# Applying dt with the mask in the scan of a hybrid decoder layer: three multiplications take other places

## The chip, the cores and the metric

The kernel runs on one core of a Trainium2 chip. The metric is device time in microseconds (us), the median of several executions; one further execution was profiled.

## The reference, cut to what matters

The layer is a feed-forward block, a mixer and a second feed-forward block, each followed by a layer norm, on 512 tokens of 1024 channels. The mixer runs sliding-window attention beside a state-space scan. Only the scan is touched. It has 4 groups of 8 heads, 64 channels a head, and goes through the tokens in 4 chunks of 128:

```python
xdt = (x * dt[..., None]).reshape(b, nc, CHUNK, G, K, P)
CB = jnp.einsum("bclgn,bcsgn->bcgls", Cc, Bc)
y_diag = jnp.einsum("bcgls,bcgkls,bcsgkp->bclgkp", CB, Lmat, xdt)
decay_states = jnp.exp(A_cum[..., -1:] - A_cum)
states = jnp.einsum("bclgn,bcgkl,bclgkp->bcgkpn", Bc, decay_states, xdt)
...
u = (y.reshape(b, L, D_INNER) * jax.nn.silu(z)).reshape(b, L, N_SSM_GROUPS, -1)
u = u * lax.rsqrt(jnp.mean(jnp.square(u), axis=-1, keepdims=True) + RMS_EPS)
u = u.reshape(b, L, D_INNER) * norm_w
y_ssm = u @ w_ssm_branch
```

So dt is a factor for each source token and head, the root is a factor for each token and group, and norm_w is a factor for each channel.

## The kernel before, in words

Every large product is computed in three matmuls of high and low halves (`mm3`, lines 124 to 126), so TensorE (PE) does three passes of 512 columns for each 128x128 block of weights. For each weight tile a copy on ScalarE (ACT) makes the high half `wh` (line 99) and a subtraction on VectorE (DVE) the low half `wl` (line 100); four buffers of each run ahead of PE.

The scan of group g is a generator, `ssd(g)`, that `weave` slips between the weight tiles of other products ("mains"): after a main, one step of the scan is issued. A step is either `decays(c)` or `turn(c - 1)` with `products(c)` and `lead(c + 1)`; so about one main, or two, lies between the decays of a chunk and its products. Each engine works its own queue strictly in the order that the scheduler of the language writes down at build time; `issue_after` keeps the scan's instructions behind the main's last matmul.

For a chunk c of a group:

- `lead` makes `ud` on GpSimd (POOL), four operations (line 572), from which PE makes the decays' exponents (lines 583 and 584).
- `decays` takes their exponentials on ACT into two tiles `seg` of four heads each (line 586), forms `cb`, the masked product of C and B (line 591), multiplies both `seg` by `cb` on DVE (line 593), makes `xdt` on DVE (line 595), and on POOL `yx` (x times d_skip, line 597) and `xds` (`xdt` times the decay to the chunk's end, line 601).
- `products` does eight matmuls of `seg` and `xdt`, one a head (line 609), then the products with the state (lines 615 and 621), adds all up on DVE, takes the sum of squares on ACT (line 632), the power -1/2 on POOL (line 634, the root `rs`), and multiplies `yx` by the root and by `normB`, norm_w broadcast to all partitions (line 635).
- `turn` transposes `yx` on PE (line 642) and splits it into the halves of `uT`, one copy on ACT and one subtraction on DVE for all four 128-column blocks (line 643 through `split_act`, lines 144 and 145). `w_ssm_tiles` multiplies `uT` by its weights later.

Tiles in PSUM for these steps come from one pool, `sm`, of four buffers. Below, "group 1, chunk 3" counts both from 0.

Of the kernel before, what the change touches and what calls it, by code (L numbers as in the profile page):

```python
# [39 lines left out]
def hybrid_layer(  # L40
# [247 lines left out]
    with tc.tile_pool(name="mix", bufs=1) as mix:  # L288
# [89 lines left out]
        with tc.tile_pool(name="attn", bufs=1) as ap:  # L378
# [37 lines left out]
            dAf = dA.rearrange("p c h -> p (c h)")  # L416
            for i, m in enumerate((upper, lower, ones)):
                nc.tensor.matmul(ps[:, i * P:(i + 1) * P], m, dAf, start=True, stop=True)
            decf = dec.rearrange("p a c h -> p (a c h)")
            nc.scalar.activation(decf, ps[:, :384], AF.Exp)  # L420
            nc.vector.tensor_scalar_mul(decf[:, :256], decf[:, :256], 0.5)
# [116 lines left out]
            k_tile(1)  # L538
            side = attention()
# [7 lines left out]
        with tc.tile_pool(name="ssd", bufs=1) as sp:  # L547
            ysum = sp.tile([P, 8, SEQ], F32, name="ysum")

            def ssd(g):  # L550
# [4 lines left out]
                normB = sp.tile([P, 512], F32, name="normB", bufs=1)  # L555
                nc.gpsimd.dma_start(normB, norm_w[0, g * 512:(g + 1) * 512].partition_broadcast(P))

                def hb(ap):
                    return ap.unsqueeze(2).broadcast_to([P, HPG, HD])

                def hv(ap):
                    return ap.rearrange("p (h d) -> p h d", h=HPG)
# [14 lines left out]
                def decays(c):  # L577
# [14 lines left out]
                    for seg in segs:  # L592
                        nc.vector.tensor_tensor(seg, seg, cb.unsqueeze(1).broadcast_to([P, 4, P]), ALU.mult)
                    xdt = sp.tile([P, 512], F32, name="xdt", bufs=2)
                    nc.vector.tensor_tensor(hv(xdt), hv(xn[:, c]), hb(dth[:, c, hs]), ALU.mult)
# [3 lines left out]
                    if c + 1 < NT:  # L599
                        xds = sp.tile([P, 512], F32, name="xds", bufs=1)  # L600
                        nc.gpsimd.tensor_tensor(hv(xds), hv(xdt), hb(dec[:, 1, c, hs]), ALU.mult)
                    st[c].update(segs=segs, xdt=xdt, yx=yx, xds=xds)

                def products(c):
                    tok = slice(c * P, (c + 1) * P)
                    segs, xdt, yx, xds = (st[c][k] for k in ("segs", "xdt", "yx", "xds"))
                    py = sm()
                    for h in range(HPG):
                        nc.tensor.matmul(py[:, h * HD:(h + 1) * HD], segs[h // 4][:, h % 4], xdt[:, h * HD:(h + 1) * HD],
                                         start=True, stop=True)  # L610
# [24 lines left out]
                    nc.vector.scalar_tensor_tensor(yx, yx, rs[:, 1:2], normB, ALU.mult, ALU.mult)  # L635

                def turn(c):
# [5 lines left out]
                    split_act((uT[:, :, 0, tok], uT[:, :, 1, tok]), ps.rearrange("p (i t) -> p i t", i=4))  # L643
# [93 lines left out]
```

## Time and profile before

| what | value |
|---|---|
| time, median of 3 runs | 1451.63 us (1449.44 to 1453.68) |
| the profiled execution's own time | 1453.2 us |
| its span, first to last instruction | 1451.5 us |
| PE busy | 1426.5 us, 98% of the span |
| DVE busy | 791.5 us, 55% |
| ACT busy | 482.1 us, 33% |
| POOL busy | 195.3 us, 13% |

The span is what the trace covers; the own time is 1.7 us longer, for what lies around the instructions. Busy times of the engines overlap. A PE that is busy for 98% leaves little room: only what the other engines make PE wait, and a lower clock of PE, can be given back.

### The profile page before, as it was taken

The page shows a single profiled execution, that of the slowest core. Times are in us where ns is not written, and L with a number is a line of the kernel's source. Part 1 is how long each engine was busy: PE and PEld are TensorE (multiplying, and loading weights), DVE is VectorE, ACT ScalarE, POOL GpSimd, SP SyncE. Part 2 cuts the span into 40 slices and gives each one's busy share as a digit, 9 for nine tenths or more (in the row PEclk, how much of TensorE's full clock was granted, in tenths as well). Part 3 has the DMA queues.
Part 4 walks back from the last instruction along what each step waited for, and adds up shares of the span by engine and source line. Part 5 has one row for each costly group of instructions (what it writes and reads, how often), then busy time and mean ns, then how long its engine had stood idle before and what let it go on. Part 6 is the DMA issues. An engine that isn't in the chain of part 4 may idle for free. (4 is left out here: it accounts for less than half of the span.)

```text
span 1451.5 us, 17121 instructions
## 1 busy us (share of the span) xinstructions
PE 1426.5 (98%) x6700; PEld 1169.7 (81%) x6700; DVE 791.5 (55%) x1246; ACT 482.1 (33%) x789; POOL 195.3 (13%) x214
## 2 busy tenths in 40 slices
PE   8999999999999999999999999999999999999997
PEld 6888888888877777887888888878878888888885
DVE  4343343233867884358659588686574434433235
ACT  4232232121346775223444234223313322322220
POOL 1000000000000000245244154261110000000001
PEclk9999999999999999999999999999999999999999
DMA  8433333323422133641231322345735333333321
GB/s 273 121 88 102 98 90 102 99 89 105 138 81 72 45 86 108 199 119 56 80 87 59 95 73 74 95 124 161 222 110 181 95 102 95 95 102 93 97 87 58
DMA packets 195633, 154.46 MB, mean 106 GB/s; under 512 B 6532, under 2 KB 169424, under 8 KB 195552
## 3 DMA queue, kind: packets, MB, share of 16 engines
q1 hardware_dynamic: 188608, 130.17, 30.1%
q0 software_dynamic: 6944, 23.19, 5.0%
q8 instruction: 53, 0.87, 0.3%
q14 instruction: 28, 0.23, 0.0%
HBM read 140.76 MB, written 12.58 MB: 106 GB/s over the span
## 5 line engine op out<-in xcount | busy, mean ns | idle before, releaser
L100 DVE TENSOR_TENSOR wl<-raw,wh 128x1024 fp32r<-128x1024 f32 (+1 forms) x233 | 299.6, 1287 | 417.3 <-ACT wh L99 412.6
L99 ACT CAST wh<-raw 128x1024 fp32r<-128x1024 f32 (+1 forms) x233 | 244.3, 1050 | 694.4 <-issue 323.7
L124 PE MATMUL acc<-xT,wh 128*128 128x512 f32 (+2 forms) x1120 | 441.9, 395 | 0.0
L125 PE MATMUL acc<-xT,wh 128*128 128x512 f32 (+2 forms) x1120 | 434.8, 388 | 0.0
L126 PE MATMUL acc<-xT,wl 128*128 128x512 f32 (+2 forms) x1120 | 433.8, 387 | 0.0
L124 PEld LDWEIGHTS acc<-xT,wh 128*128 128x128 f32 x1120 | 210.9, 188 | 44.5 <-issue 3.2
L125 PEld LDWEIGHTS acc<-xT,wh 128*128 128x128 f32 x1120 | 210.7, 188 | 44.2 <-issue 3.3
L126 PEld LDWEIGHTS acc<-xT,wl 128*128 128x128 f32 x1120 | 210.4, 188 | 43.0 <-issue 0.2
L124 PE MATMUL dn<-wh,hT 128*128 128x512 f32 x352 | 137.2, 390 | 0.0
L125 PE MATMUL dn<-wl,hT 128*128 128x512 f32 x352 | 137.1, 390 | 0.0
L126 PE MATMUL dn<-wh,hT 128*128 128x512 f32 x352 | 136.9, 389 | 0.0
L160 POOL TENSOR_TENSOR sts<-sts,cols 128x1 f32<-128x1 f32 x12 | 11.9, 990 | 719.9 <-DVE sts L159 719.9
L572 POOL TENSOR_TENSOR ud<-upper,dAr 128x512 fp32r<-128x512 f32 x64 | 86.4, 1378 | 104.2 <-PE sm L584 104.2
L239 DVE TENSOR_TENSOR t<-t,acc 128x512 f32<-128x512 f32 x44 | 30.2, 687 | 111.6 <-PE acc L126 111.4
L125 PEld LDWEIGHTS dn<-wl,hT 128*128 128x128 f32 x352 | 66.1, 188 | 13.7
L126 PEld LDWEIGHTS dn<-wh,hT 128*128 128x128 f32 x352 | 66.1, 188 | 13.6
L124 PEld LDWEIGHTS dn<-wh,hT 128*128 128x128 f32 x352 | 66.1, 188 | 13.6
L124 PE MATMUL z<-wh,xT 128*128 128x512 f32 x128 | 51.5, 402 | 0.0
L124 PE MATMUL acc<-uT,wh 128*128 128x512 f32 x128 | 50.5, 395 | 0.0
L126 PE MATMUL z<-wh,xT 128*128 128x512 f32 x128 | 49.9, 390 | 0.0
L125 PE MATMUL z<-wl,xT 128*128 128x512 f32 x128 | 49.9, 390 | 0.0
L126 PE MATMUL acc<-uT,wl 128*128 128x512 f32 x128 | 49.9, 390 | 0.0
(212 smaller groups left out, 1691.8 us busy)
## 6 DMA issues: line engine op xcount, KB each, us to landing
raw<-in_w_in_dram SPq DMA_DIRECT2D x66, 512.0 KB, 3.7
raw<-in_ffn_w_gate_dram SPq DMA_DIRECT2D x44, 512.0 KB, 3.8
raw<-in_ffn_w_up_dram SPq DMA_DIRECT2D x44, 512.0 KB, 3.7
raw<-in_ffn_w_down_dram SPq DMA_DIRECT2D x44, 512.0 KB, 3.6
raw<-in_w_ssm_branch_dram SPq DMA_DIRECT2D x16, 512.0 KB, 3.4
raw<-in_w_attn_branch_dram SPq DMA_DIRECT2D x8, 512.0 KB, 4.1
raw<-in_w_out_dram SPq DMA_DIRECT2D x8, 512.0 KB, 4.4
r<-in_x_dram SPq DMA_DIRECT2D x8, 256.0 KB, 5.7
```

The costliest lines, as they stand in the source:

```text
L99: nc.scalar.copy(h[:, :n], raw[:, :n])
L100: nc.vector.tensor_tensor(l[:, :n], raw[:, :n], f(h[:, :n]), ALU.subtract)
L124: nc.tensor.matmul(ps, lh, rh, start=start, stop=False)
L125: nc.tensor.matmul(ps, lh, rl, start=False, stop=False)
L126: cur["mm"] = nc.tensor.matmul(ps, ll, rh, start=False, stop=stop)
L160: nc.gpsimd.tensor_tensor(mv[:, 3:4], mv[:, 2:3], mhalf[:, 0:1], ALU.pow)
L239: nc.vector.tensor_tensor(t, t, pu, ALU.mult)
L572: nc.gpsimd.tensor_tensor(ud[:, i], upper.unsqueeze(1).broadcast_to([P, 4, P]), f(dAr[:, i, c, h0:h0 + 4]).unsqueeze(2).broadcast_to([P, 4 ...
```

## The change

Three multiplications of the scan move. First, dt: `xdt` is no longer made. The eight heads' masks are multiplied one by one by dt (a factor of each partition) and by `cb` in one DVE instruction a head, and the matmuls take `xn` itself; the factor that `xds` needs goes into `dec[:, 1]` once, ahead of the scan. Second, norm_w: its four broadcast loads are gone; its 16 rows of 128 are loaded once in the attention stage, transposed by PE and kept as columns (`nwc`), and `turn` multiplies by a column while it splits, so the one copy and one subtraction of 512 columns become four of each of 128. Third, the root: `yx` is multiplied by it on ACT instead of on DVE.

```diff
+            rows = ap.tile([P, SEQ], F32, tag="ta", name="ta", bufs=2)
+            nc.gpsimd.dma_start(rows[:16, :P], norm_w[0].rearrange("(t p) -> t p", p=P))
...
-            nc.vector.tensor_scalar_mul(decf[:, :256], decf[:, :256], 0.5)
+            nc.vector.tensor_scalar_mul(dec[:, 0], dec[:, 0], 0.5)
+            nc.vector.scalar_tensor_tensor(dec[:, 1], dec[:, 1], 0.5, dth, ALU.mult, ALU.mult)
...
+            nwc = heads[:, 0]
+            ps = sm()
+            with tc.issue_after(cur["mm"].ins):
+                nc.tensor.transpose(ps[:, :16], rows[:16, :P], ident[:16, :16])
+            nc.scalar.copy(nwc[:, :16], ps[:, :16])
...
-                normB = sp.tile([P, 512], F32, name="normB", bufs=1)
-                nc.gpsimd.dma_start(normB, norm_w[0, g * 512:(g + 1) * 512].partition_broadcast(P))
...
-                    for seg in segs:
-                        nc.vector.tensor_tensor(seg, seg, cb.unsqueeze(1).broadcast_to([P, 4, P]), ALU.mult)
-                    xdt = sp.tile([P, 512], F32, name="xdt", bufs=2)
-                    nc.vector.tensor_tensor(hv(xdt), hv(xn[:, c]), hb(dth[:, c, hs]), ALU.mult)
+                    for h in range(HPG):
+                        s_, h_ = segs[h // 4][:, h % 4], g * HPG + h
+                        nc.vector.scalar_tensor_tensor(s_, s_, dth[:, c, h_:h_ + 1], cb, ALU.mult, ALU.mult)
...
-                        nc.gpsimd.tensor_tensor(hv(xds), hv(xdt), hb(dec[:, 1, c, hs]), ALU.mult)
+                        nc.gpsimd.tensor_tensor(hv(xds), hv(xn[:, c]), hb(dec[:, 1, c, hs]), ALU.mult)
...
-                        nc.tensor.matmul(py[:, h * HD:(h + 1) * HD], segs[h // 4][:, h % 4], xdt[:, h * HD:(h + 1) * HD],
+                        nc.tensor.matmul(py[:, h * HD:(h + 1) * HD], segs[h // 4][:, h % 4], xn[:, c, h * HD:(h + 1) * HD],
                                          start=True, stop=True)
...
-                    nc.vector.scalar_tensor_tensor(yx, yx, rs[:, 1:2], normB, ALU.mult, ALU.mult)
+                    nc.scalar.activation(yx, yx, AF.Copy, scale=rs[:, 1:2])
...
-                    split_act((uT[:, :, 0, tok], uT[:, :, 1, tok]), ps.rearrange("p (i t) -> p i t", i=4))
+                    for i in range(4):
+                        w_, p_ = nwc[:, 4 * g + i:4 * g + i + 1], ps[:, i * P:(i + 1) * P]
+                        nc.scalar.activation(uT[:, i, 0, tok], p_, AF.Copy, scale=w_)
+                        nc.vector.scalar_tensor_tensor(uT[:, i, 1, tok], p_, w_, f(uT[:, i, 0, tok]), ALU.mult, ALU.subtract)
```

In the changed kernel's lines, 578 is the `ud` of line 572, 592 the exponentials of 586, 597 the `cb` of 591, 600 the new mask multiplication, 602 and 606 the `yx` and `xds` of 597 and 601, 637 to 639 the sum of squares to the root of 632 to 634, 640 the multiplication by the root on ACT, 650 and 651 the two halves of the split.

The scheduler also writes down another order at some places. Three of them matter.

The first is POOL's queue where the scan goes from group 1 to group 2. Before, the root of group 1's chunk 2 (`rs_5246`) stands ahead of the four `ud` of group 2's chunk 0:

```order
L597 TENSOR_TENSOR yx_5322<-xn_3350,heads_66 128x512
L634 TENSOR_TENSOR rs_5246<-rs_5246,cols_90 128x1
L572 TENSOR_TENSOR ud_5618<-upper_74,dAr_2621 128x512 x2
L572 TENSOR_TENSOR ud_5621<-upper_74,dAr_2621 128x512 x2
L597 TENSOR_TENSOR yx_5676<-xn_4977,heads_66 128x512
```

In the changed kernel the same root is `rs_5274`:

```order
L602 TENSOR_TENSOR yx_5354<-xn_3356,heads_66 128x512
L578 TENSOR_TENSOR ud_5660<-upper_74,dAr_2621 128x512 x2
L578 TENSOR_TENSOR ud_5663<-upper_74,dAr_2621 128x512
L639 TENSOR_TENSOR rs_5274<-rs_5274,cols_90 128x1
L578 TENSOR_TENSOR ud_5663<-upper_74,dAr_2621 128x512
L602 TENSOR_TENSOR yx_5722<-xn_4985,heads_66 128x512
```

The root moved behind three of the four `ud`; the same happens from group 0 to group 1 and from group 2 to group 3.

The second is ACT's queue at the same point, group 1's chunk 3. Before, the sum of squares of chunk 2 is followed by the exponentials of chunk 3:

```order
L632 ACTIVATE yo_5247,rs_5246<-yx_5169 128x512
L302 ACTIVATE BT_5289<-acc_5264,cols_90 128x512
L326 COPY xn_4977<-sm_5298 128x4x128
L586 ACTIVATE seg_5307<-sm_5304 128x512
L586 ACTIVATE seg_5312<-sm_5309 128x512
L99 CAST wh_5477<-raw_5475 128x1024
```

In the changed kernel the multiplication by that root stands between them:

```order
L637 ACTIVATE yo_5275,rs_5274<-yx_5191 128x512
L302 ACTIVATE BT_5317<-acc_5292,cols_90 128x512
L326 COPY xn_4985<-sm_5326 128x4x128
L640 ACTIVATE yx_5191<-yx_5191,rs_5274 128x512
L592 ACTIVATE seg_5335<-sm_5332 128x512
L592 ACTIVATE seg_5340<-sm_5337 128x512
L307 ACTIVATE th_5322<-BT_5317 128x512
L99 CAST wh_5551<-raw_5549 128x1024
```

The multiplication, which needs POOL's root, moved in ahead of chunk 3's exponentials.

The third is DVE's queue in group 3, from chunk 1's multiplication by z (line 629, now 634) to chunk 2's masks. Before:

```order
L595 TENSOR_TENSOR xdt<-xn,dth 128x512
L629 TENSOR_TENSOR yx<-yx,zs 128x512
L633 TENSOR_SCALAR rs<-rs 128x1
L635 SCALAR_TENSOR_TENSOR yx<-yx,rs,normB 128x512
L100 TENSOR_TENSOR wl<-raw,wh 128x1024
L681 SCALAR_TENSOR_TENSOR ysum<-tg,ysum 128x512
L591 TENSOR_TENSOR cb<-sm,quarter 128x128
L682 TENSOR_TENSOR ysum<-ysum,m_7427 128x512
L593 TENSOR_TENSOR seg<-seg,cb 128x512 x2
```

In the changed kernel:

```order
L634 TENSOR_TENSOR yx<-yx,zs 128x512
L638 TENSOR_SCALAR rs<-rs 128x1
L100 TENSOR_TENSOR wl<-raw,wh 128x1024
L689 SCALAR_TENSOR_TENSOR ysum<-tg,ysum 128x512
L597 TENSOR_TENSOR cb<-sm,quarter 128x128
L690 TENSOR_TENSOR ysum<-ysum,m_7559 128x512
L600 SCALAR_TENSOR_TENSOR seg<-seg,dth,cb 128x128 x8
```

`xdt` and the multiplication by the root have left this stretch, and the two masks have become eight. In most chunks whose main is a convolution tile (groups 0 to 2, chunks 1 to 3), the eight stand apart: one, then the convolution's third step (line 305), three, its last step (line 308, which waits for a tanh on ACT), and four.

## Rows read from the trace of the kernel before

**Rows 1.** The page's first part: busy us, share of span, instructions.

```profile
PE 1426.5 (98%) x6700; PEld 1169.7 (81%) x6700; DVE 791.5 (55%) x1246; ACT 482.1 (33%) x789; POOL 195.3 (13%) x214
```

**Rows 2.** PE's waits from 620 to 1000 us: us, times, longest.

```profile
PE sm L609 <- DVE seg L593: 2.8, 4, 1.2
PE sm L642 <- DVE yx L635: 0.6, 1, 0.6
```

**Rows 3.** PE's timeline: start, length, line, [idle before and releaser].

```profile
680.19 2.02 PE L615 MATMUL sm<-prev,CT 128*128 128x512 f32 x2
...
683.86 0.39 PE L125 MATMUL acc<-xT,wh 128*128 128x512 f32 x1
...
952.45 1.08 PE L615 MATMUL sm<-prev,CT 128*128 128x512 f32 x2
...
954.45 0.39 PE L125 MATMUL acc<-xT,wh 128*128 128x512 f32 x1
...
968.09 2.00 PE L609 MATMUL sm<-xdt,seg 128*128 128x64 f32 x16 [1.16 <-DVE seg L593]
969.93 1.69 PE L615 MATMUL sm<-prev,CT 128*128 128x512 f32 x2
...
973.55 0.45 PE L125 MATMUL acc<-xT,wh 128*128 128x512 f32 x1
```

**Rows 4.** Two stretches by window: busy times of engines, PEclk, DMA.

```profile
680.20:683.60 3.40, 3.40 (x7) 1.40 (x6) 3.40 (x5) 1.48 (x3) 0.00 (x0) 0.51 0.30 87
...
970.30:973.70 3.40, 3.40 (x6) 1.50 (x5) 3.40 (x6) 0.00 (x0) 0.66 (x2) 0.50 0.76 258
```

**Rows 5.** Timelines of POOL and DVE ahead of those two stretches.

```profile
670.09 5.08 POOL L572 TENSOR_TENSOR ud<-upper,dAr 128x512 fp32r<-128x512 f32 x4 [0.95 <-PE sm L584]
675.13 0.55 POOL L634 TENSOR_TENSOR rs<-rs,cols 128x1 f32<-128x1 f32 x1
...
675.71 0.75 DVE L635 SCALAR_TENSOR_TENSOR yx<-yx,rs,normB 128x512 f32<-128x512 f32 x1 [2.52 <-POOL rs L634]
...
961.03 1.53 DVE L635 SCALAR_TENSOR_TENSOR yx<-yx,rs,normB 128x512 f32<-128x512 f32 x1 [0.67 <-POOL rs L634]
...
967.36 1.28 DVE L593 TENSOR_TENSOR seg<-seg,cb 128x512 f32<-128x512 f32 x2
```

**Rows 6.** Groups of instructions: count, busy us, mean ns, idle before.

```profile
L593 DVE TENSOR_TENSOR seg<-seg,cb 128x512 f32<-128x512 f32 x32 | 32.6, 1036 | 0.5
L595 DVE TENSOR_TENSOR xdt<-xn,dth 128x512 f32<-128x512 f32 x16 | 15.0, 945 | 1.3 <-DMA m1d<-ta 1.3
L635 DVE SCALAR_TENSOR_TENSOR yx<-yx,rs,normB 128x512 f32<-128x512 f32 x16 | 12.8, 799 | 11.3 <-POOL rs L634 11.3
L302 ACT ACTIVATE ct<-acc,cols 128x512 f32<-128x512 f32 x16 | 12.3, 771 | 0.1
L145 DVE TENSOR_TENSOR uT<-sm,uT 128x512 fp32r<-128x512 f32 x16 | 10.9, 680 | 1.4 <-ACT uT L144 1.4
L476 ACT ACTIVATE pr<-pr,smls 128x128 f32<-128x128 f32 x16 | 6.2, 392 | 0.0
L408 DVE SCALAR_TENSOR_TENSOR tmp<-tmp 128x128 f32<-128x128 f32 x7 | 2.0, 288 | 0.2
```

**Rows 7.** Timeline at 646.5 us, group 0's chunk 0, POOL and DVE.

```profile
645.24 1.48 POOL L572 TENSOR_TENSOR ud<-upper,dAr 128x512 fp32r<-128x512 f32 x1
645.75 1.52 DVE L593 TENSOR_TENSOR seg<-seg,cb 128x512 f32<-128x512 f32 x1
```

**Rows 8.** PE's timeline in group 1's chunk 1.

```profile
761.39 1.90 PE L609 MATMUL sm<-xdt,seg 128*128 128x64 f32 x16
763.13 1.08 PE L615 MATMUL sm<-prev,CT 128*128 128x512 f32 x2
```

**Rows 9.** Timelines of POOL, ACT and PE in group 1's chunk 3.

```profile
794.37 4.93 POOL L572 TENSOR_TENSOR ud<-upper,dAr 128x512 fp32r<-128x512 f32 x4 [0.84 <-PE sm L584]
...
794.57 1.10 ACT L586 ACTIVATE seg<-sm 128x512 f32<-128x512 f32 x2
...
801.16 1.90 PE L609 MATMUL sm<-xdt,seg 128*128 128x64 f32 x16
```

More of the change, by code (lines that the diff above doesn't have):

```diff
@@ L600, in decays @@
                         xds = sp.tile([P, 512], F32, name="xds", bufs=1)
-                        nc.gpsimd.tensor_tensor(hv(xds), hv(xdt), hb(dec[:, 1, c, hs]), ALU.mult)
-                    st[c].update(segs=segs, xdt=xdt, yx=yx, xds=xds)
+                        nc.gpsimd.tensor_tensor(hv(xds), hv(xn[:, c]), hb(dec[:, 1, c, hs]), ALU.mult)
+                    st[c].update(segs=segs, yx=yx, xds=xds)
                 def products(c):
                     tok = slice(c * P, (c + 1) * P)
-                    segs, xdt, yx, xds = (st[c][k] for k in ("segs", "xdt", "yx", "xds"))
+                    segs, yx, xds = (st[c][k] for k in ("segs", "yx", "xds"))
                     py = sm()
                     for h in range(HPG):
-                        nc.tensor.matmul(py[:, h * HD:(h + 1) * HD], segs[h // 4][:, h % 4], xdt[:, h * HD:(h + 1) * HD],
+                        nc.tensor.matmul(py[:, h * HD:(h + 1) * HD], segs[h // 4][:, h % 4], xn[:, c, h * HD:(h + 1) * HD],
                                          start=True, stop=True)
```

## The prediction, made before the changed kernel ran

> **What bounds the kernel now.** The page comes first: PE is busy for 98% of the span and DVE, which the change touches most, for 55% [rows 1]. An instruction that leaves DVE or comes to ACT therefore costs or gives time only where PE waits for its result. So the second view is PE's own waits in the stretch of the scan, about 620 to 1000 us [rows 2]: 2.8 us in all for the masks of line 593, in four waits, and 0.6 us for a multiplication by the root. The third is PE's clock. After two of these waits the granted clock falls to its lower level, 1.2 GHz, for some 3.4 us, at 680 and at 970 us [rows 4]. What that costs is read from the same three products at full clock: from line 615 to the second matmul of the next main takes 954.45 - 952.45 = 2.00 us, but 683.86 - 680.19 = 3.67 us and 973.55 - 969.93 = 3.62 us in the two slow stretches [rows 3]; 1.65 us lost in each. Together the scan loses 2.8 + 0.6 + 3.3 = 6.7 us, and that is all that any rearrangement of the scan's side work can give back, 0.46% of the time.
>
> Why PE waited there is in the fourth view, the queues of DVE and POOL ahead of the stretches [rows 5]. At 673 us (group 0, chunk 2) POOL worked off four `ud` in 5.08 us before the root, so DVE stood 2.52 us in front of line 635, with the masks behind it. At 961 us (group 3, chunk 2) line 635 waited 0.67 us and then took 1.53 us, and the masks were through only at 968.64; PE, which was ready after its transposes, waited 1.16 us [rows 3, 5].
>
> **The change, part by part.** *DVE's sum.* Out go 32 masks of 1036 ns, 16 `xdt` of 945, 16 multiplications of 799 and 16 subtractions of 680: 71.3 us. In come 128 masks and 64 subtractions of 128 columns. The nearest row is 288 ns, where POOL is idle [rows 6]: 192 x 0.288 = 55.3 us, so DVE loses 16 us. If the small ones slow down beside POOL as the large ones do (1036 against 680), they take 0.44 us each, 84 us, and DVE gains 13 us. Neither end matters as a sum, since DVE idles 45% of the time; what matters is each chunk's order.
>
> *ACT's sum.* 16 multiplications of at most 0.77 us (line 302, which also takes its factor from a tile) and 64 small copies of about 0.39 us, the row of 128 columns [rows 6], come to 37 us, less what the 16 large copies took. ACT is busy for 482 of 1451 us, and the weights' copies run tiles ahead; this is hidden, and would cost something only if `wh` came late by more than the lead of four buffers.
>
> *PE and the queues of transfers.* One transpose of 16 columns in the attention stage, about 0.1 us; its rows are asked for on POOL's queue behind the sinks, some mains before PE needs them, so I take no wait. Four issues of `normB` leave POOL's queue; nothing on PE waited for them. SP's queue is unchanged.
>
> *Group 3, chunk 2.* Line 635 leaves DVE, which frees about 0.67 + 1.45 us, but the next instruction needs `wh`, so I count 1.4 us. The masks then begin near 966, and eight at 0.29 us with one wait for POOL (below) end at 969.0 instead of 968.64; yet PE can begin at 966.8 with the first, because it takes a head in (763.13 - 761.39) / 8 = 0.22 us [rows 8]. It ends at about 969.1 instead of 969.8: 0.7 us gained. The wait of 1.16 us in one piece is gone, and I expect the full clock here: 1.6 us more.
>
> *Group 0, chunk 2.* DVE no longer waits for the root; ACT does. POOL still comes to it behind the `ud`, at 675.7 [rows 5] or, since a state product now stands among them, up to 1.2 us later. Line 640 adds 0.77 us. Behind it on ACT wait the tanh of the convolution and, through DVE's line 308, the last four masks. They end between 678.5 and 680.1, where the last mask was done at 679.2. So this place gives back between 1 us with its slow stretch, 2.7 us in all, and a loss of 1; I take 0.5 us and let the slow stretch stay. Group 0's chunk 1 gains on the root and loses on the pieces: 0.
>
> *Masks beside POOL.* A mask takes 1.52 us while a `ud` runs: the `ud` ended at 646.72 and the mask at 647.27, 0.55 us later, so the mask did all its work after POOL had finished [rows 7]. Then a mask of a quarter of the size waits just as long for POOL and only works less. The Trainium skill, page "SBUF — State Buffer", section "SBUF: two separate sides", says so: a DVE instruction with two SBUF inputs and a GpSimd instruction that reads SBUF exclude each other for the whole instruction. It speaks against the change, for eight pieces can be held eight times where two were held twice, and this trace agrees in the 1.52 us. By the ratio of the rows (0.44 us a piece) chunk 1 of groups 1 and 2 would not wait at all; held by POOL's last two `ud` and by `yx`, three waits of up to 1 us, the last masks come at about 763.2, and PE needs them from 761.39 + 7 x 0.22 = 762.9 [rows 8]. I take 0.3 us at each of the two, 0.6 us. Nothing lost is the lower end, 0.9 us each the upper.
>
> *Chunk 3 of groups 0 to 2.* Here the change makes a new wait. Before, the exponentials ran at 794.57, 6.6 us ahead of PE's need at 801.16 [rows 9]. Now they stand behind line 640, that behind the root, and that behind three `ud`, which PE frees at 794.37. A `ud` that no mask holds up takes 1.48 - 0.55 = 0.93 us [rows 7], and none does, as DVE itself waits for the exponentials: the root is then there at 797.7, line 640 done at 798.5, the first exponential at 799.0, and eight masks with two convolution steps between them, 8 x 0.29 + 2 x 0.68 = 3.7 us, end at 802.7. PE needs the last at 801.16 + 1.54 = 802.7: no wait, and no slack. At the row's mean, 4.93 / 4 = 1.23 us, all comes 0.9 us later. I take 0.3 us at three places, nearer to the free `ud`: 0.9 us. Behind these masks on DVE wait the `wl`, which have a lead of several mains.
>
> **The sum.** -0.7 - 1.6 - 0.5 + 0.6 + 0.9 + 0.1 = -1.2 us. Against the profiled execution's own 1453.2 us that is 1452.0; the median of the runs shown is 1451.6, so I forecast 1450.4.
>
> **The rivals.** *All waits vanish.* With masks that come early everywhere, both slow stretches go too: -6.7 us, 1444.9. For it speaks that all PE's losses in the scan are waits for DVE [rows 2]; against it that at 676 us the root itself is late, whoever waits for it.
>
> *Nothing to be seen.* The waits trade places and both slow stretches stay: -0.7 - 0.5 + 1.5 + 0.1 = +0.4, 1452.0. For it speaks PE's 98%.
>
> *ACT blocked by the root, slower.* In chunk 3 of groups 0 to 2 each `ud` takes 1.48 us, as in [rows 7]; the root comes at 799.4, the masks end at 804.4, PE waits 1.7 us three times, and as after the waits of [rows 3] the clock falls each time: 3 x (1.7 + 1.65) = 10.0 instead of the 0.9 in the sum, 1459.5. It decides from about 4 us for the three `ud` on, where PE's wait reaches the 1.16 us of [rows 3].
>
> *Pieces held by POOL.* Every piece is held that finds a POOL instruction beside it: 0.9 us at five chunks (1 and 2 of groups 1 and 2, chunk 1 of group 0), 4.5 instead of 0.6, 1454.3. Against it speaks that POOL has only two `ud` and `yx` to hold them with in that time. The rule of the Trainium skill's page "SBUF — State Buffer", above, would do this at its worst.
>
> **How the numbers follow.** Chances: the forecast 0.45, all waits vanish 0.15, nothing to be seen 0.17, ACT blocked 0.13, pieces held 0.10. A measurement of this kernel tells about 0.3%, 4.4 us, from no change. Faster by more are the first rival and the lower edge of the forecast, 0.19; slower by more most of ACT blocked and a part of pieces held, 0.13; the rest, 0.68, is the same. The range of 1445 to 1456 reaches from the first rival to beyond held pieces and leaves out most of ACT blocked; the forecast's own range is 1447 to 1453.
>
> **What would show it.** Right: no wait of PE near 968 and no lower clock there; `xdt` gone and DVE's busy time within 16 us below and 13 us above 791.5; in chunk 3 of groups 0 to 2 ACT idle for 3 to 4 us in front of line 640, released by POOL. Wrong: the lower clock in chunk 3 of any group; a mask of line 600 with a mean far above 0.44 us; or a wait of PE that is new, for a buffer of `sm` held by the slower split, or for `wl`.

## The result, and the profile of the changed kernel

The changed kernel is slower: 1460.8 us (median of 4 runs, 1460.24 to 1464.43) against 1452.62 us of the kernel before on the same chip, a ratio of 1.0069 with a 95% interval of 1.0056 to 1.0082. The forecast was 1450.4, and the range ended at 1456. The profiled execution took 1460.24 us, its span is 1458.5 us.

The page's first part of the changed kernel, busy us, share of the span and instructions:

```profile
PE 1428.2 (98%) x6701; PEld 1170.9 (80%) x6701; DVE 787.5 (54%) x1359; ACT 505.9 (35%) x854; POOL 187.2 (13%) x211
```

DVE does 4.0 us less than before and ACT 23.8 us more [rows 1]; both stay near half of the span or below, so no engine's sum explains 7 us. PE's own waits do. The view of [rows 2], the same stretch, for the changed kernel:

```profile
PE z L124 <- DVE CT L305: 5.5, 2, 2.8
PE sm L614 <- DVE seg L600: 2.8, 7, 0.8
PE sm L647 <- ACT yx L640: 0.5, 1, 0.5
```

The second and third line are the old ones in other places. The first is new: twice, the first matmul of a `z` tile waits 2.8 us for a convolution step of the tile `CT` on DVE. The windows show what follows it, and answer to [rows 4] (busy us of PE, PEld, DVE, ACT and POOL, then PEclk, DMA share, GB/s):

```profile
802.40:805.80 3.40, 3.19 (x9) 2.54 (x10) 2.56 (x9) 0.88 (x2) 0.00 (x0) 0.51 0.00 0
904.80:908.20 3.40, 3.30 (x10) 2.64 (x11) 2.45 (x8) 0.99 (x2) 0.00 (x0) 0.51 0.02 5
800.00:802.30 2.30, 0.00 (x0) 0.00 (x0) 1.38 (x2) 1.38 (x3) 1.66 (x2) 1.00 0.00 0
681.10:684.50 3.40, 3.40 (x14) 2.13 (x14) 3.40 (x5) 0.37 (x1) 0.00 (x0) 1.00 0.41 96
979.20:982.60 3.40, 3.40 (x13) 2.23 (x12) 3.40 (x6) 1.11 (x4) 2.18 (x4) 1.00 0.68 232
```

The third window is the wait itself: PE does nothing. Behind it, and at the same place 102 us later, the granted clock is at the lower level (0.51). The last two windows lie where the low stretches of before lay, behind the matmuls of line 614 in chunk 2 of groups 0 and 3 (the second of them is 9 us later in this kernel); the clock there is 1.00, so the two low stretches are gone. Together the windows show that, in this execution, the low clock moved from chunk 2 of groups 0 and 3 to chunk 3 of groups 1 and 2.

How much each chunk costs is read from the start of its last decay matmul (line 584, now 590), with which a chunk begins on PE. A step runs from the row above to its own row, over the chunks that are left out too; of the two long steps that end at chunk 3 of groups 1 and 2, the difference lies in chunk 1:

| last decay matmul starts | before | after | step, before | step, after | difference |
|---|---|---|---|---|---|
| group 0, chunk 1 | 657.97 | 658.13 | | | |
| group 0, chunk 2 | 670.08 | 671.23 | 12.11 | 13.10 | +1.0 |
| group 0, chunk 3 | 690.24 | 689.50 | 20.16 | 18.27 | -1.9 |
| group 1, chunk 0 | 740.25 | 740.60 | 50.01 | 51.10 | +1.1 |
| group 1, chunk 3 | 794.36 | 795.11 | 54.11 | 54.51 | +0.4 |
| group 2, chunk 0 | 837.65 | 842.88 | 43.29 | 47.77 | +4.5 |
| group 2, chunk 3 | 891.72 | 897.40 | 54.07 | 54.52 | +0.45 |
| group 3, chunk 0 | 929.59 | 939.80 | 37.87 | 42.40 | +4.5 |
| group 3, chunk 2 | 960.39 | 970.57 | 30.80 | 30.77 | 0.0 |
| group 3, chunk 3 | 979.55 | 986.76 | 19.16 | 16.19 | -3.0 |

The two steps of +4.5 hold more than the whole loss: 2.78 us of waiting and the 1.65 us that a low stretch costs [rows 3] are 4.43. They are chunk 3 of group 1 and of group 2. (In chunk 3 of group 0, the +1.1, PE waits 0.58 us for masks and 0.52 us for the transposes.) The timelines of the first (start, length, engine, line; in brackets the idle time before and its releaser) answer to [rows 9] and [rows 5], POOL, ACT, DVE and PE after one another. The first line is the first of the three `ud` of the second line by itself:

```profile
795.12 2.02 POOL L578 TENSOR_TENSOR ud<-upper,dAr 128x512 fp32r<-128x512 f32 x1 [7.72 <-PE sm L590]
795.12 4.02 POOL L578 TENSOR_TENSOR ud<-upper,dAr 128x512 fp32r<-128x512 f32 x3 [7.72 <-PE sm L590]
799.10 0.55 POOL L639 TENSOR_TENSOR rs<-rs,cols 128x1 f32<-128x1 f32 x1
799.62 1.04 POOL L578 TENSOR_TENSOR ud<-upper,dAr 128x512 fp32r<-128x512 f32 x1
...
793.94 1.05 ACT L99 CAST wh<-raw 128x1024 fp32r<-128x1024 f32 x1 [3.97 <-PE acc L125]
794.89 0.63 ACT L637 ACTIVATE yo<-yx 128x512 f32<-128x512 f32 x1
...
799.68 0.72 ACT L640 ACTIVATE yx<-yx,rs 128x512 f32<-128x512 f32 x1 [2.93 <-POOL rs L639]
800.31 1.06 ACT L592 ACTIVATE seg<-sm 128x512 f32<-128x512 f32 x2
...
792.53 0.69 DVE L634 TENSOR_TENSOR yx<-yx,zs 128x512 f32<-128x512 f32 x1
795.02 1.23 DVE L100 TENSOR_TENSOR wl<-raw,wh 128x1024 fp32r<-128x1024 f32 x1 [1.79 <-ACT wh L99]
796.16 0.15 DVE L638 TENSOR_SCALAR rs<-rs 128x1 f32<-128x1 f32 x1
796.42 1.53 DVE L305 SCALAR_TENSOR_TENSOR CT<-acc,cols,CT 128x511 f32<-128x511 f32 x2
800.92 0.88 DVE L600 SCALAR_TENSOR_TENSOR seg<-seg,dth,cb 128x128 f32<-128x128 f32 x1 [2.97 <-ACT seg L592]
801.73 0.73 DVE L305 SCALAR_TENSOR_TENSOR CT<-acc,cols,CT 128x509 f32<-128x509 f32 x1
802.39 0.86 DVE L600 SCALAR_TENSOR_TENSOR seg<-seg,dth,cb 128x128 f32<-128x128 f32 x3
...
803.83 1.13 DVE L600 SCALAR_TENSOR_TENSOR seg<-seg,dth,cb 128x128 f32<-128x128 f32 x4
...
802.61 0.77 PE L124 MATMUL z<-wh,xT 128*128 128x512 f32 x1 [2.78 <-DVE CT L305]
803.17 0.63 PE L125 MATMUL z<-wl,xT 128*128 128x512 f32 x1
...
806.38 1.90 PE L614 MATMUL sm<-xn,seg 128*128 128x64 f32 x16
```

Read from top to bottom it is one chain. Three `ud` take 4.02 us of POOL; the root comes behind them, at 799.65. ACT stood 2.93 us in front of line 640, and the exponentials are behind it. DVE stood 2.97 us in front of the first mask, and the third step of the convolution of `CT` is behind that mask: it ends at 802.46. The accumulator of `CT` in PSUM is read by this step; PE's next `z` tile wants an accumulator and starts at 802.61. The masks, for which the prediction had looked, are done at 804.96, and PE comes to them at 806.38 without a wait, because it had lost the time already. `z` runs its matmuls in 0.63 us at the low clock, against 0.39 to 0.40 at the full one.

The groups of instructions that answer to [rows 6], the fields as there:

```profile
L578 POOL TENSOR_TENSOR ud<-upper,dAr 128x512 fp32r<-128x512 f32 x64 | 79.5, 1269 | 134.7 <-PE sm L590 132.8 <-DMA m1d<-ta 2.0
L600 DVE SCALAR_TENSOR_TENSOR seg<-seg,dth,cb 128x128 f32<-128x128 f32 x128 | 57.3, 503 | 8.5 <-ACT seg L592 7.9
L650 ACT ACTIVATE uT<-sm,heads 128x128 fp32r<-128x128 f32 x64 | 23.4, 366 | 40.7 <-DVE uT L651 39.9 <-PE sm L647 0.7
L651 DVE SCALAR_TENSOR_TENSOR uT<-sm,heads,uT 128x128 fp32r<-128x128 f32 x64 | 21.8, 340 | 8.0 <-ACT uT L650 8.0
```

A mask takes 503 ns in the mean, above both bounds of the prediction (0.288 and 0.44 us). The split's pieces cost about what was foreseen (366 ns against 0.39 us on ACT, 340 ns between the two bounds on DVE).

### The profile page after: what moved, and what is told of

Its sections match the earlier page's. It is cut to its first block, busy times and chain, and to the rows that moved or that the text cites. A ratio compares the mean times of both kernels' runs of the same rounds, so it can differ in the third digit from the quotient of the medians.

```text
span 1458.5 us, 17321 instructions
## 1 busy us (share of the span) xinstructions
PE 1428.2 (98%) x6701; PEld 1170.9 (80%) x6701; DVE 787.5 (54%) x1359; ACT 505.9 (35%) x854; POOL 187.2 (13%) x211
## 5 line engine op out<-in xcount | busy, mean ns | idle before, releaser
L100 DVE TENSOR_TENSOR wl<-raw,wh 128x1024 fp32r<-128x1024 f32 (+1 forms) x233 | 291.3, 1252 | 422.9 <-ACT wh L99 421.3
L578 POOL TENSOR_TENSOR ud<-upper,dAr 128x512 fp32r<-128x512 f32 x64 | 79.5, 1269 | 134.7 <-PE sm L590 132.8
L600 DVE SCALAR_TENSOR_TENSOR seg<-seg,dth,cb 128x128 f32<-128x128 f32 x128 | 57.3, 503 | 8.5 <-ACT seg L592 7.9
```

The source lines that it names most:

```text
L100: nc.vector.tensor_tensor(l[:, :n], raw[:, :n], f(h[:, :n]), ALU.subtract)
L578: nc.gpsimd.tensor_tensor(ud[:, i], upper.unsqueeze(1).broadcast_to([P, 4, P]), f(dAr[:, i, c, h0:h0 + 4]).unsqueeze(2).broadcast_to([P, 4 ...
L600: nc.vector.scalar_tensor_tensor(s_, s_, dth[:, c, h_:h_ + 1], cb, ALU.mult, ALU.mult)
```

## The experiments

Fifteen kernels ran, each timed in five rounds beside the kernel before on the same chip, where that took 1452.4 to 1452.8 us. All compute the whole layer. "Root first" is the edit of e1. Theory R, the chain above, stood against three others: that ScalarE's wait as such is what costs (its narrow form), that the small masks are too slow (M), and that the eight pieces of the split hold buffers (S).

| run | changed against the kernel after | median us | ratio to before, 95% interval |
|---|---|---|---|
| e1_root_first | POOL: root ahead of the `ud` | 1454.8 | 1.0015 [1.0007, 1.0024] |
| e2_root_back | root's multiplication on DVE | 1468.6 | 1.0111 [1.0097, 1.0125] |
| e3_dt_back | dt and masks as before | 1462.71 | 1.0069 [1.0055, 1.0082] |
| e4_norm_alone | both: the weight in the split alone is left | 1460.53 | 1.0053 [1.0040, 1.0066] |
| e5_conv_first | DVE: masks behind the convolution | 1460.18 | 1.0055 [1.0041, 1.0069] |
| e6_dt_alone | dt in the masks alone is left | 1461.7 | 1.0063 [1.0049, 1.0076] |
| e7_rf_dt | e3, root first | 1450.85 | 0.9989 [0.9979, 0.9998] |
| e8_rf_norm | e4, root first | 1453.7 | 1.0011 [1.0000, 1.0022] |
| e9_ud_late | e1, next group's `ud` later still | 1452.0 | 0.9998 [0.9989, 1.0008] |
| e10_rf_dtalone | e6, root first | 1456.87 | 1.0034 [1.0022, 1.0047] |
| e11_rf_dt_exp | e7, root's multiplication behind the exponentials | 1450.25 | 0.9988 [0.9978, 0.9998] |
| e12_rf_dt_conv | e7, masks behind the convolution | 1452.54 | 1.0004 [0.9994, 1.0014] |
| e13_sums_first | casts of weights behind the sum of squares | 1565.87 | 1.0783 [1.0768, 1.0798] |
| e14_ul_dt | e7, next group's `ud` later still | 1449.38 | 0.9981 [0.9972, 0.9990] |
| e15_sums_dt | e3 and e13 | 1574.13 | 1.0840 [1.0825, 1.0855] |

### The root's place on POOL (e1)

```diff
-                    nc.gpsimd.tensor_tensor(rs[:, 1:2], rs[:, 0:1], mhalf[:, 0:1], ALU.pow)
+                    roots.append(nc.gpsimd.tensor_tensor(rs[:, 1:2], rs[:, 0:1], mhalf[:, 0:1], ALU.pow))
...
+                        with tc.issue_after(roots[-2].ins) if len(roots) > 1 else ExitStack():
-                        for i in range(2):
+                            for i in range(2):
...
```

> Only GpSimd's order is changed against the kernel after: in chunk 3 of each group the root stands ahead of all four ud multiplications, as it did in the kernel before, and not behind three of them. Theory R (the root stands 4.0 us behind three ud, the exponentials stand behind its multiplication on ScalarE, the third convolution step of CT behind the masks on VectorE, and the z tiles lack a PSUM buffer): both waits of the z matmuls and both slow-clock stretches of groups 1 and 2 go, 2 x 4.5 us, and about 1 us of late masks in group 0: 1460.8 - 10 = 1451, between 1449 and 1453. Theory M (the 128 small masks are too slow, 503 ns each with VectorE's port held by GpSimd): the time stays at 1459 to 1462. Theory S (the eight small operations of the split hold the sm buffers): stays as well.

The queues of PE, DVE and ACT are the same, instruction by instruction, as in the changed kernel; only POOL's differs. 1460.8 became 1454.8. The first line of PE's waits in the scan:

```profile
PE sm L616 <- DVE seg L602: 4.0, 8, 0.9
```

The waits of `z` are gone, as Theory R had it; M and S alone would have kept 1459 or more. But the time is 1.8 us above the expected 1449 to 1453, and the masks make PE wait more than before, 4.0 us in eight waits. The timelines of DVE and POOL of e1 in group 1's chunk 3, where PE then waits 0.80 us for the masks:

```profile
802.14 2.57 DVE L602 SCALAR_TENSOR_TENSOR seg<-seg,dth,cb 128x128 f32<-128x128 f32 x3
...
805.23 1.92 DVE L602 SCALAR_TENSOR_TENSOR seg<-seg,dth,cb 128x128 f32<-128x128 f32 x4
...
799.37 4.14 POOL L580 TENSOR_TENSOR ud<-upper,dAr 128x512 fp32r<-128x512 f32 x4
803.47 1.09 POOL L608 TENSOR_TENSOR xds<-xn,dec 128x512 f32<-128x512 f32 x1
```

While POOL runs, three masks need 2.57 us. In the changed kernel the same three took 0.86 us, at 802.39, when POOL was through with its `ud` and `xds`. So it is the root's place in e1 that brings the masks and the `ud` together. That POOL holds the masks became Theory P, tried in e9.

### The parts alone, with POOL's order as it came (e2, e3, e4)

The edit of e2, which e4 has as well:

```diff
-                    nc.scalar.activation(yx, yx, AF.Copy, scale=rs[:, 1:2])
+                    nc.vector.tensor_scalar_mul(yx, yx, rs[:, 1:2])
```

The core of the edit of e3, which e4 has as well (the matmuls and `xds` take `xdt` again):

```diff
-                    for h in range(HPG):
-                        s_, h_ = segs[h // 4][:, h % 4], g * HPG + h
-                        nc.vector.scalar_tensor_tensor(s_, s_, dth[:, c, h_:h_ + 1], cb, ALU.mult, ALU.mult)
+                    for seg in segs:
+                        nc.vector.tensor_tensor(seg, seg, cb.unsqueeze(1).broadcast_to([P, 4, P]), ALU.mult)
+                    xdt = sp.tile([P, 512], F32, name="xdt", bufs=2)
+                    nc.vector.tensor_tensor(hv(xdt), hv(xn[:, c]), hb(dth[:, c, hs]), ALU.mult)
```

> The root's multiplication is back on VectorE (one operation of 512 columns with the root alone, without the norm's weight); the rest is the kernel after, and GpSimd still has the root behind three ud in chunk 3 of groups 1 and 2. Theory R in its narrow form (A: what costs is that ScalarE is blocked, so that the exponentials come late): the z waits go and the time falls to about 1451. Theory R in its wide form (whoever multiplies by the root is blocked for 4 us; here VectorE, with the second and third convolution steps of CT right behind): the z waits stay within 0.7 us of what they are, 1458 to 1461. Theory M: 1459 to 1462 too, but with the z waits gone it would have to show the time in the masks.

> dt is back in a product of its own on VectorE (512 columns) and the masks are two of 512 columns with C times B alone; the split with the weight and the root on ScalarE are those of the kernel after, and the root stands behind three ud. Theory R: the z waits stay, 1457 to 1461. Theory M: the small masks were the cost, so the time goes back to 1451 to 1453 and the z waits are gone. Theory S: stays at 1459 to 1461.

> Only the middle part of the change is left: the weight of the norm in the split of the transposed rows; dt and masks are as before, and the root's multiplication is on VectorE (without the weight). GpSimd has the root behind three ud here as well, so that Theory R in its wide form expects the z waits to stay and 1456 to 1461, its narrow form (ScalarE blocked) about 1452, Theory M 1452, and Theory S (the split's eight small operations) 1455 or more without z waits.

All three keep the waits of `z`, and all stay slow. The first line of PE's waits in the scan, of e2:

```profile
PE z L124 <- DVE CT L305: 5.9, 2, 3.0
```

The same line of e3:

```profile
PE z L124 <- DVE CT L305: 6.9, 2, 3.5
```

And of e4, where only the split is left:

```profile
PE z L124 <- DVE CT L305: 6.3, 2, 3.2
```

So it isn't ScalarE's wait as such (the narrow form falls with e2 and e4), nor the small masks (M falls with e3, which has none). The split is in all three, so S is not tested here; it fell with e1, and e7 below has the split and is not slower than the kernel before. With the multiplication back on DVE the same root holds DVE directly, as its timeline in e2 shows, and two steps of `CT` stand behind it:

```profile
804.96 1.26 DVE L640 TENSOR_SCALAR yx<-yx,rs 128x512 f32<-128x512 f32 x1 [2.52 <-POOL rs L639]
806.14 0.73 DVE L305 SCALAR_TENSOR_TENSOR CT<-acc,cols,CT 128x510 f32<-128x510 f32 x1
```

That e2 would be 8 us slower than the changed kernel was expected by no theory. It has nine waits for masks besides, 4.7 us, and a granted clock of 0.50 to 0.80 in five windows of 3.4 or 4 us, where the changed kernel has two. Its waits in the scan are 2.4 us longer in all (11.2 against 8.8 us), and three more low stretches of 1.65 us would make 5 us more, as an estimate: some 7 of the 9.1 us by which the spans differ. Why its masks come so late was not followed.

### The PSUM buffer (e5)

```diff
-                nc.vector.scalar_tensor_tensor(ct[:, d:], ps[:, :SEQ - d], cols[:, i:i + 1], ct[:, d:], ALU.mult, ALU.add)
+                cur["conv"] = nc.vector.scalar_tensor_tensor(ct[:, d:], ps[:, :SEQ - d], cols[:, i:i + 1], ct[:, d:], ALU.mult, ALU.add)
...
-                        nc.vector.scalar_tensor_tensor(s_, s_, dth[:, c, h_:h_ + 1], cb, ALU.mult, ALU.mult)
+                        with tc.issue_after(cur["conv"].ins):
+                            nc.vector.scalar_tensor_tensor(s_, s_, dth[:, c, h_:h_ + 1], cb, ALU.mult, ALU.mult)
```

> The kernel after with one thing moved: on VectorE each chunk's masks stand behind the last convolution step of the tile that is being convolved, so that the CT step no longer waits behind a mask. The root still stands behind three ud, and the exponentials are as late as they are. Theory R in full (the price of groups 1 and 2 is the PSUM buffer that the late third CT step holds): both z waits and both slow-clock stretches go, the masks are late by up to 1 us in the main behind: 1460.8 - 2 x (2.8 + 1.65) + 2 x 1 = 1454, between 1451.5 and 1456. If it is the late exponentials themselves that cost (the matmuls of py waiting for masks), or another holder of the PSUM buffer: 1459 to 1462.

A miss. The waits of `z` are gone, so it was this step that they hung on; but the median is 1460.18, as if nothing had been done. The profiled execution was the shortest of its six (1457.53). PE's waits of e5 in the scan, the first line:

```profile
PE sm L615 <- DVE seg L601: 5.1, 8, 1.2
```

Two windows of e5, each behind one of its two longest waits (columns as above):

```profile
805.00:809.00 4.00, 4.00 (x15) 2.80 (x16) 4.00 (x11) 0.73 (x2) 0.00 (x0) 0.69 0.17 55
906.00:910.00 4.00, 3.71 (x19) 2.95 (x20) 4.00 (x10) 0.74 (x2) 0.08 (x1) 1.00 0.11 27
```

PE, no longer held by `z`, waits 1.2 us for the masks, in both chunks, and in this execution the clock fell behind one of the two waits. So the late exponentials have two ways to PE, and closing one opens the other. That the second way accounts for the whole median is argued from this one trace.

### Each part with the root first (e7, e8, e10, and e6 beside them)

e6 is the kernel before with that part of the change's diff that concerns dt (`dec`, the masks, `xds`, the matmuls); e7, e8 and e10 are e3, e4 and e6 with the edge of e1:

```diff
+                        with tc.issue_after(roots[-2].ins) if len(roots) > 1 else ExitStack():
```

> The kernel before with only dt moved into the masks (eight masks of 128 columns a chunk and no product of x and dt); the split, the weight and the root are as before, and GpSimd has the root ahead of the ud in groups 1 and 2. Theory R with the small masks as a second cost (a mask costs about 1.1 us where GpSimd runs an operation, against 0.34 where it doesn't, as in chunk 3 of the run with the root first): no z waits, +1.0 in chunk 1 of group 0, +0.4 in chunk 1 of groups 1 and 2, +1.6 in chunk 3 of both, a gain of about 0.5 to 3 in chunk 2 of groups 0 and 3 each: about 1454, between 1451 and 1457. If dt in the mask were what moves the root: z waits and 1458 or more.

> The split with the weight and the root on ScalarE as after; dt and the masks as before; and GpSimd's root ahead of the ud. Theory R with the small masks as a second cost: neither wait is left in chunk 3 of groups 1 and 2, and the gains of the run without dt in chunk 2 of group 0 (2.8) and of group 3 (2.9) stay: 1452.7 - 5 = 1448, between 1446 and 1451. If the root on ScalarE costs by itself, also when the root is early: 1453 or more, with a wait for exponentials.

> Only the weight in the split, with GpSimd's root ahead of the ud; the root's multiplication on VectorE, dt and masks as before. Theory R: no z waits, and chunk 2 of groups 0 and 3 give back 2.9 and 2.5: 1447 to 1451. If the eight small operations of the split cost by themselves (Theory S): 1453 or more, with waits for a buffer of sm or for the uT halves.

> dt alone in the masks (the kernel before otherwise), with the root ahead of the ud in group 0 as well. With dt alone the root of chunk 1 of group 0 stood behind four ud and its multiplication held VectorE's masks (a wait of 2.7 us for the root, and 1.4 us of py for a mask). If that order is what dt alone paid for in group 0 (2.8 us in each of chunks 2 and 3): 1461.7 - 5 = 1457, between 1453.5 and 1459. If it is the eight masks themselves: 1460 to 1462.

Each fell: e3 from 1462.71 to 1450.85, e4 from 1460.53 to 1453.7, e6 from 1461.7 to 1456.87. e7 is at the upper end of the interval that was expected, e8 2.7 us above the end of it: in e8 `z` still waits twice for 1.4 us, and the transposes 2.4 us for the root's multiplication on DVE; no wait is for a buffer, as S would have it. e6 was a miss by 4.7 us: it has no waits of `z`, but in group 0 it meets the old stall of [rows 5] with eight masks behind it. The timelines of POOL and DVE in e6:

```profile
676.73 0.55 POOL L634 TENSOR_TENSOR rs<-rs,cols 128x1 f32<-128x1 f32 x1
...
677.31 0.75 DVE L635 SCALAR_TENSOR_TENSOR yx<-yx,rs,normB 128x512 f32<-128x512 f32 x1 [2.72 <-POOL rs L634]
...
681.16 1.39 DVE L595 SCALAR_TENSOR_TENSOR seg<-seg,dth,cb 128x128 f32<-128x128 f32 x5
```

With the root first in group 0 too (e10) 4.8 of these 9 us came back, as expected; 4.4 us stay, and PE still waits 3.9 us for the small masks there.

### The masks beside POOL (e9)

```diff
-                        with tc.issue_after(roots[-2].ins) if len(roots) > 1 else ExitStack():
+                        with tc.issue_after(roots[-2 if c else -1].ins) if len(roots) > 1 else ExitStack():
```

> The kernel with the root first, and in addition the four ud of the next group's first chunk stand behind the last root of a group on GpSimd, so that they no longer run beside the masks of chunk 3; the orders of TensorE, VectorE and ScalarE are the same as with the root first. Theory P (a small mask is held for the length of a GpSimd operation that runs beside it, 1.13 us against 0.34): the masks of chunk 3 in groups 1 and 2 end 2 us sooner, the wait of 0.8 us in front of the second half of the py matmuls goes, and each of these chunks gives back about 1.6: 1454.8 - 3.3 = 1451.5, between 1450 and 1453.5. If eight masks simply are too many, or VectorE's order holds them: unchanged, 1454 to 1456.

As expected: 1452.0, the time of the kernel before, with all three edits in it and, against the changed kernel, only POOL's order different. The timelines of DVE (the masks in group 1's chunk 3) and POOL in e9:

```profile
799.38 0.87 DVE L602 SCALAR_TENSOR_TENSOR seg<-seg,dth,cb 128x128 f32<-128x128 f32 x3
...
800.83 1.14 DVE L602 SCALAR_TENSOR_TENSOR seg<-seg,dth,cb 128x128 f32<-128x128 f32 x4
...
797.14 1.04 POOL L608 TENSOR_TENSOR xds<-xn,dec 128x512 f32<-128x512 f32 x1
802.46 1.04 POOL L604 TENSOR_TENSOR yx<-xn,heads 128x512 f32<-128x512 f32 x1 [4.27 <-PE sm L649]
```

The same three masks take 0.87 us with POOL idle that took 2.57 us in e1, the same four 1.14 instead of 1.92. The page "SBUF — State Buffer" of the Trainium skill, section "SBUF: two separate sides", says that a DVE instruction with two SBUF inputs and a GpSimd instruction that reads SBUF exclude each other for a whole instruction. The trace agrees, with 2.57 us against 0.87 us for the three masks, whose two large operands both lie in SBUF.

### What is left to win (e11, e12, e14)

All three start from e7. e11 moves the multiplication, e12 has e5's edge for the two large masks, e14 that of e9. The edit of e11:

```diff
-                    nc.scalar.activation(yx, yx, AF.Copy, scale=rs[:, 1:2])
+                    st[c]["rs"] = rs
...
+                    with tc.issue_after(cur["exp"].ins):
+                        nc.scalar.activation(yx, yx, AF.Copy, scale=rs[:, 1:2])
```

> The best so far (dt as before, split with the weight, root on ScalarE, GpSimd's root first), with the root's multiplication behind the exponentials of the chunk on ScalarE. The two waits of 0.7 us that z has left in chunk 3 of groups 1 and 2 come from exponentials 0.7 us behind that multiplication, if Theory R holds down to small sizes: they go, 1450.9 - 1.9 = 1449, between 1447.5 and 1451. If something else sets the remaining wait: unchanged at 1450.9.

> The best so far with the two masks of a chunk behind the last convolution step on VectorE. Theory R: the PSUM buffer of CT comes free 1.5 us sooner, z no longer waits in chunk 3 of groups 1 and 2, the masks are no later than the py matmuls: 1450.9 - 1.9 = 1449, between 1447.5 and 1451. If the masks come too late for py by this: 1451 to 1453.

> The split with the weight and the root on ScalarE, dt and masks as before, the root ahead of the ud and the next group's ud behind the last root of a group. The 0.7 us that z still waits in chunk 3 of groups 1 and 2 with the root first come from the product of x and dt, which stands ahead of a CT step and takes 1.4 us beside a ud against 0.7 alone (Theory P): without the ud the waits go and the chunks give back 0.95 each: 1450.5 - 1.9 = 1448.6, between 1447 and 1451. Otherwise unchanged, 1450 to 1452.

e11 moved the median by 0.6 us, which the intervals do not tell from nothing, and kept both waits of `z`, 0.7 us each: its mechanism was wrong. e12 was no gain: the waits of `z` fell from 1.4 to 0.5 us in all, but the transposes waited 2.8 us for the root's multiplication on ACT. DVE's timeline of e11 shows what stands ahead of the step of `CT`:

```profile
793.74 1.41 DVE L602 TENSOR_TENSOR xdt<-xn,dth 128x512 f32<-128x512 f32 x1
```

And the same product in DVE's timeline of e14, where no `ud` runs beside it:

```profile
792.98 0.68 DVE L602 TENSOR_TENSOR xdt<-xn,dth 128x512 f32<-128x512 f32 x1
```

e14 has the lowest median, 1449.38, 0.19% below the kernel before (0.9981, 0.9972 to 0.9990). The product became short as foreseen and the waits of `z` fell from 0.7 to 0.2 us each; the waits for the root's multiplication went from 0.4 us in e7 to 0.8 us. Its interval overlaps those of e7 and e11, so a gain over them isn't shown. PE's waits in e14:

```profile
PE sm L649 <- ACT yx L642: 0.8, 2, 0.6
PE z L124 <- DVE CT L306: 0.5, 2, 0.2
```

### Why the root came late (e13, e15)

```diff
-        nc.scalar.copy(h[:, :n], raw[:, :n])
-        nc.vector.tensor_tensor(l[:, :n], raw[:, :n], f(h[:, :n]), ALU.subtract)
+        with tc.issue_after(sums[-1][0].ins) if sums else ExitStack():
+            nc.scalar.copy(h[:, :n], raw[:, :n])
+        with tc.issue_after(sums[-1][1].ins) if sums else ExitStack():
+            nc.vector.tensor_tensor(l[:, :n], raw[:, :n], f(h[:, :n]), ALU.subtract)
```

> The kernel after with all three edits, and nothing set for GpSimd: instead the casts of the weights (ScalarE) and their low halves (VectorE) that are loaded behind a chunk stand behind that chunk's sum of squares and the step ahead of the root. GpSimd's order follows by itself, and has the root ahead of the ud in chunk 3 of groups 1 and 2. Theory C (the root stands behind the ud because the sum of squares stands behind a cast of weights that waits for its buffer: it starts 0.6 us ahead of the end of the decay matmuls, in the kernel before 2.7 us ahead): no z waits, the root as early as in the kernel before, and what is left are the masks beside the ud: 1452.5 to 1456, most likely 1454. If the cast isn't what holds the chain, or the weights now come late: 1459 or more.

> dt and masks as before, the split with the weight, the root on ScalarE, and the sums of squares ahead of the casts of weights. Theory C: no z waits, and the gains of chunk 2 in groups 0 and 3 stay: 1447 to 1451. If the weights come late by it: 1453 or more.

e15 has the same edit on e3. Both fail to answer. The edge holds every cast, not the one that was in the way, and PE runs out of weights, as e13's waits show:

```profile
PE acc L128 <- ACT wh L102: 59.6, 13, 6.9
PE z L128 <- ACT wh L102: 13.9, 3, 5.5
```

## Why the prediction was wrong, and where it was right

**The step that failed** is that on chunk 3 of groups 0 to 2: +0.9 us was foreseen for the three together, +1.1, +4.5 and +4.5 were measured. It saw the chain (exponentials behind line 640, that behind the root, that behind three `ud`), and failed in two of its members.

*The price of the `ud`.* It was taken as 0.93 us each, on the ground that no mask holds a `ud` up there, as DVE itself waits for the exponentials. Three took 4.02 us. The second and third took 1.0 us each, near the 0.93. The first took 2.02 us, beside a `wl` that DVE had begun 0.1 us before it (795.02, 1.23 us): DVE was not idle yet. So the ground failed, not the price of a free `ud`, although that was worked out from a loose reading: the 0.55 us that [rows 7] leave the mask after POOL is less than the shortest mask of this kind takes, 0.68 us, so it cannot have done all its work then.

The rival "ACT blocked by the root" named about 4 us for the three as the point from which it decides, and that is where they came out; its chance stood at 0.13. Its 1459.5 lies 1.3 us below the result, but in part by luck: it had PE wait for the masks, 1.7 us in three chunks, where PE waited for `z`, 2.8 us in two.

The root was late also at its other end. Before, the corresponding lines of DVE were:

```profile
791.21 0.69 DVE L629 TENSOR_TENSOR yx<-yx,zs 128x512 f32<-128x512 f32 x1
792.75 0.15 DVE L633 TENSOR_SCALAR rs<-rs 128x1 f32<-128x1 f32 x1 [0.85 <-ACT yo L632]
```

In the changed kernel the sum of squares ran at 794.89, behind a cast of weights that waited 3.97 us, 0.22 us ahead of the chunk's last decay matmul at 795.11; before it ran at 792.00, 2.36 us ahead of that at 794.36. The root's last input, line 638, stands on DVE behind the `wl` of that same cast. From the end of the multiplication by z to the end of this step it is 3.1 us (793.22 to 796.31), and it was 1.0 us (791.90 to 792.90): 2.1 us come from the cast and its `wl`, the same `wl` beside which the first `ud` ran. In e1, with the root first on POOL, the root was there at 799.41, 1.83 us after the decay matmul at 797.58, in the changed kernel 4.54 us after it (799.65 - 795.11). So, against e1, the three `ud` add 2.7 us, and the rest is lateness that was there ahead of them. Why the scheduler puts the cast there was not settled (e13).

*What waits behind the masks.* The prediction named only the `wl`. In the order ("one, then the convolution's third step") stood what it didn't follow: that step reads PSUM, and the `z` tile of the same main wants the accumulator. So PE stood from 799.83 (802.61 - 2.78) on, long before it comes to the masks. e5 takes this step out of the chain and the median stays, with PE waiting 1.2 us for the masks instead; e1 brings the root forward and gives 6.0 us back. So the root's lateness was the graver of the two.

**The clock.** "The lower clock in chunk 3 of any group" was named as a sign of being wrong; it is there twice, each time behind PE's idle 2.8 us, and costs about 1.7 us (the step's 4.48 less the 2.78 of waiting). An idle time of that length does not always bring it: in e4 the clock behind a wait of 3.17 us was 1.00, and behind the next one, 3.16 us, 0.54.

**Group 3, chunk 2.** -2.3 foreseen, -3.0 measured. Right in its mechanism: no wait of PE for these masks, and the clock stays at 1.00. **Group 0, chunk 2.** -0.5 foreseen, -1.9 measured: the root was as late as expected (ACT waited 3.1 us for it), but the low stretch, which was left in the sum, didn't come. In e1 it is there again (0.57 from 683.00 to 686.40 us), so this gain of one execution can't be credited to the change. **Group 0, chunk 1.** 0 foreseen, +1.0 measured, the rival "pieces held by POOL": three masks took 2.56 us there. **Chunk 1 of groups 1 and 2.** 0.6 foreseen, 0.40 + 0.45 measured. **The sums.** DVE's busy time went down by 4.0 us, within the 16 below and 13 above; ACT's work was hidden but for the order of its queue. The buffers of `sm` and the split's pieces held nobody.

The sum of the measured steps is 1.0 - 1.9 + 1.1 + 0.4 + 4.5 + 0.45 + 4.5 - 3.0 = 7.05 us, and the spans differ by 7.0. The rival at the other end, that all waits vanish, came about in no run: the kernel with the lowest median, e14, has waits of 1.3 us left and gives 3.0 us, not 6.7.

**What is shown and what is not.** Shown: changing POOL's order alone, with the other queues untouched, takes back the whole loss. Putting the root ahead of the `ud`, as the kernel before had it, gives 6.0 us (1460.8 to 1454.8). Keeping the `ud` off the masks as well, an order that neither kernel had, gives the rest (to 1452.0). Shown as well: dt in the masks doesn't pay with the root first (e1 with it 1454.8, e7 without it 1450.85). The late order of the root comes with the part of the change that concerns norm_w: e4, which has that part alone, has its sum of squares behind the cast (794.52, behind a cast that waited 4.10 us) and its root behind three `ud`, and e6, without that part, has neither in chunk 3 of group 1. Only argued: that within this part it is the split in pieces that does it. Open: what the kernel would take without the cast in that place (e13 and e15 failed to answer), and why the clock falls behind some waits and not behind others of the same length.

## What to carry to other kernels

An instruction that takes over a wait hands it to all that stands behind it on its queue: follow the order there to the first instruction that gives back a buffer of PSUM or of the critical engine, not only to the next user of the same data. Take a duration together with its neighbours: a free `ud` was priced nearly right, but what the other engine runs beside it in the new order was not looked up. And before a change is given up, see whether an order that came with it, not the change, is what costs: here the old place of one root a group on one queue was worth 6.0 us (1460.8 to 1454.8), and a better place of four `ud` another 2.8 us (to 1452.0).

## What the runs showed of the hardware

- In these runs a POOL instruction slows a DVE instruction whose operands are all in SBUF, by count more than by size: three masks of 128 columns took 0.87 us with POOL idle (e9) and 2.57 us beside `ud` and `xds` (e1), `xdt` of 512 columns 0.68 us (e14) and, beside `ud`, 1.41 us (e11). A step of the convolution, which reads one of its two large operands from PSUM, took 0.73 us beside a `ud` (e1) and 0.74 us without (e9).
- POOL is slowed in its turn, but not by every instruction of DVE: a `ud` took 2.02 us beside a `wl` of 1.23 us, and the next two 1.0 us each (the changed kernel). Four took 4.14 us in e1, beside steps of `CT` and the small masks.
- Two waits of the same length can end differently: behind 1.2 us the granted clock was 0.69 in one window and 1.00 in the other of the same execution (e5), behind 0.9 us in group 0's chunk 2 it was 0.57 in e1 and 1.00 in e9, and behind 3.2 us it was 1.00 and 0.54 in e4.
